# A decoder layer on eight cores: the ScalarE half of layer-norm jobs moved behind the next unit's PSUM copies, down partials added straight from PSUM, wide loads, and an fp16 copy of x1

## Chip, cores, metric

One Trainium2 chip, one program on all 8 cores, in two dies (cores 0 to 3 and 4 to 7). The metric is the device time of one execution in microseconds (us), on the slowest of the cores. Executions fall into two states: in the slow one a die has a visibly lower granted TensorE clock and the time is some per cent longer.

In the text, TensorE is the matmul engine (PE in the profile), VectorE is DVE, ScalarE is ACT, GpSimd is POOL. PSUM is the memory that the matmuls write, divided into banks; SBUF is the other memory on the chip, from which the engines work. In the profile lines `sp` is a PSUM bank and `arena` is SBUF. A line "PE sp L1295 <- ACT arena L1423" means that TensorE, at line 1295 of the kernel, waited for what ScalarE does at line 1423.

## The reference, cut to what matters

```python
def layer_norm(x, g, b):
    xf = x.astype(jnp.float32)
    mu = xf.mean(-1, keepdims=True)
    var = jnp.square(xf - mu).mean(-1, keepdims=True)
    return ((xf - mu) * lax.rsqrt(var + LN_EPS) * g + b).astype(x.dtype)

def swiglu(x, w_up, w_down):
    gate, up = jnp.split(jnp.einsum('bsd,df->bsf', x, w_up), 2, axis=-1)
    return jnp.einsum('bsf,fd->bsd', jax.nn.silu(gate) * up, w_down)

# reference(), one layer; SEQ = 16384, D_MODEL = 2048, D_FF = 5632
mix = token_mixer(x, ...)                         # attention, w_out
x = layer_norm(ALPHA * x + mix, ln1_g, ln1_b)     # "x1"
x = layer_norm(ALPHA * x + swiglu(x, w_up, w_down), ln2_g, ln2_b)
```

The change lies in what follows `token_mixer`: the two layer norms and the feed-forward product.

## The kernel before

A core has 2048 tokens and does the feed-forward part for two halves of 1024 (`st`), and in each half for two halves of the hidden width (`g`). One `(st, g)` has 22 **units**, each giving two 128x512 tiles of the hidden layer h, and then a **down stage** of eight **steps**, each giving 2 x 2 tiles of the output. So there are four down stages, in order: stage 1 (`st`=0, `g`=0) adds x1 to its products and stores the partial as `z2s`; stage 2 (0, 1) reads that partial back and finishes it; stages 3 and 4 do the same for the second half.

Products are done in half-size blocks, seven instead of eight, of sums of weights and of activations that VectorE makes: a unit is 7 x 8 = 56 matmuls into four PSUM banks, a step 7 x 11 = 77.

Between the units **jobs** are run, two in a unit: in `st` = 0 the last layer-norm operations of x1 for the second half, in `st` = 1 those of the output of the first half. There are 32 jobs in each half, so 16 units carry them. A job is two VectorE operations (subtract the mean, multiply by the inverse deviation) and one ScalarE operation (scale and bias), then a store:

```python
def ln1_tile(ss, st, n, hh, z, bz):
    ...
    S_.dve(lambda: nc.vector.tensor_tensor(out=z, in0=z, in1=mu, op=ALU.subtract), [bz, bmu], [bz])
    S_.dve(lambda: nc.vector.tensor_tensor(out=z, in0=z, in1=rs, op=ALU.mult), [bz, brs], [bz])
    ...
    S_.act(lambda: nc.scalar.activation(out=z, in_=z, **args), [bz, k.bsmall], [bz])
    S_.dma("act", k.x1s_d[n, :, c0:c0 + 512], z, [bz], [b], "x1s")
```

`S_.dve`, `S_.act` and `S_.dma` append to an engine's program; the lists are the buffers read and written, from which the waits follow. Each engine works through its program in order. A unit (cut):

```python
if fl == 0 and g == 0:
    ...                      # first unit of a half: 64 plain matmuls, then sums of x1 on VectorE
    run_jobs(2)
    continue
...
P("4", s, True, True)                                   # P: 8 matmuls into a bank
S_.act(lambda ...: nc.scalar.activation(out=v4, in_=pa, func=AF.Copy), [ba_], [b4])   # first copy
P("5", s + 1, True, True)
S_.act(lambda ...: nc.scalar.activation(out=v5, in_=pb, func=AF.Copy), [bb_], [b5])   # second copy
P("1", s + 2, True, True)
tt(v5, b5, pd, bd_, v5, b5, ALU.subtract)
P("2", s + 3, True, True)
tt(v4, b4, pc, bc_, v4, b4, ALU.add)
...                                                     # weight sums P, Q of the next unit
P("3", s + 1, False, True)     # adds to the bank of the second copy: must wait for it
...
if kh:
    ...                        # every second unit: four more sums, over h
...                            # weight sum R of the next unit
run_jobs(2)
```

A down step and the reload of x1 for the second half (cut):

```python
P("4", s, True, True, cs)
acc_x(*q21, pa, ba_)                       # q..: the loaded partial tiles, in SBUF
P("5", s + 1, True, True, cs)
S_.act(lambda pb=pb: nc.scalar.activation(out=t5, in_=pb, func=AF.Copy), [bb_], [bt5])
P("1", s + 2, True, True, cs)
tt(t5, bt5, pd, bd_, t5, bt5, ALU.subtract)
P("2", s + 3, True, True, cs)
tt(q21[0], q21[1], pc, bc_, q21[0], q21[1], ALU.add)
...
P("3", s + 1, False, True)
acc_x(*q12, pb, bb_)
P("7", s, False, True)
tt(t11, bt11, pa, ba_, t5, bt5, ALU.add)
acc_x(*q11, t11, bt11)                     # SBUF + SBUF
P("6", s + 3, False, True)
tt(t5, bt5, t5, bt5, pc, bc_, ALU.subtract)
tt(t5, bt5, pb, bb_, t5, bt5, ALU.add)
acc_x(*q22, t5, bt5)                       # SBUF + SBUF

def load_x1(st, b):                        # fp32 in DRAM, cast to fp16 by the transfer
    S_.dma("pool", xall[:, b, :, :], k.x1s_d[8 * kh:8 * kh + 8, :, c0:c0 + 512].rearrange("n p t -> p n t"), ...)
```

The softmax here doesn't subtract the row's maximum and nothing guards it: scores larger than these inputs give would overflow.

Of the kernel before, what the change touches and what calls it, by code (L numbers as in the profile page):

```python
# [8 lines left out]
F32 = mybir.dt.float32  # L9
# [3 lines left out]
ALU = mybir.AluOpType  # L13
# [202 lines left out]
def build(debug=False):  # L216
# [34 lines left out]
    k.x1s_d = dt("x1s", [KC, 128, TOK], F32, kind="Internal").ap()  # L251
    k.z2s_d = dt("z2s", [KC, 128, TOK], F32, kind="Internal").ap()
# [868 lines left out]
def phase3(k):  # L1121
# [73 lines left out]
    bx1s = {}  # L1195

    def ln1_tile(ss, st, n, hh, z, bz):
        (mu, bmu), (rs, brs) = ss["stat"][hh]
        S_.dve(lambda: nc.vector.tensor_tensor(out=z, in0=z, in1=mu, op=ALU.subtract), [bz, bmu], [bz])
        S_.dve(lambda: nc.vector.tensor_tensor(out=z, in0=z, in1=rs, op=ALU.mult), [bz, brs], [bz])  # L1200
        args = dict(func=AF.Identity, bias=k.lnp[:, 1, n:n + 1], scale=k.lnp[:, 0, n:n + 1])
        if st == 0:
            key = (RAW[n // 8, hh], n % 8)
            S_.act(lambda: nc.scalar.activation(out=xb[key], in_=z, **args), [bz, k.bsmall], [bxb[key]])
        S_.act(lambda: nc.scalar.activation(out=z, in_=z, **args), [bz, k.bsmall], [bz])
        b = Buf("x1s%d_%d_%d" % (st, n, hh))
        c0 = st * TS + hh * 512
        S_.dma("act", k.x1s_d[n, :, c0:c0 + 512], z, [bz], [b], "x1s")
        bx1s[(st, n, hh)] = b

    def load_x1(st, b):
        (kh, hh), = [e for e in RAW if RAW[e] == b]
        c0 = st * TS + hh * 512
        S_.dma("pool", xall[:, b, :, :], k.x1s_d[8 * kh:8 * kh + 8, :, c0:c0 + 512].rearrange("n p t -> p n t"),
               [bx1s[(st, n, hh)] for n in range(8 * kh, 8 * kh + 8)], [bxb[b, c] for c in range(8)], "x1l")

    fins = []
    jobs = []

    def run_jobs(n):  # L1220
        for _ in range(min(n, len(jobs))):
            jobs.pop(0)()

    for st in range(2):
# [19 lines left out]
        for si, (n, hh) in enumerate(steps):  # L1244
# [15 lines left out]
            if st == 1:  # L1260
                run_jobs(3 if si < 2 else 2 if si % 2 else 1)
                if not jobs:
                    wgate(k, 0, 0)
# [69 lines left out]
    for st in range(2):  # L1333
        for g in range(2):
# [7 lines left out]
                     [xslot(10), xslot(11), xslot(5), WB + 11264] + [WB + i * 2048 for i in range(4)]  # L1342
            zr = {}

            def load_xq(p):
                q = []
                for i in range(4):
                    n, hh = 2 * p + i // 2, i % 2
                    c0 = st * TS + hh * 512
                    o = zslots[4 * p + i] if last else wslot(6 - 4 * (p % 2) + i)  # L1350
                    v, b = slot("xq%d%d_%d_%d" % (st, g, n, hh), o)
                    if g == 0:
                        S_.dma("sp", v, k.x1s_d[n, :, c0:c0 + 512], [bx1s[(st, n, hh)]], [b], "xq")
                    else:
                        S_.dma("sp", v, k.z2s_d[n, :, c0:c0 + 512], [bz2s[(st, n, hh)]], [b], "xq")
                    q.append((v, b))
                    zr[n, hh] = (v, b)
                return q

            for fl in range(FG):  # L1360
# [4 lines left out]
                if fl == FG - 1:  # L1365
                    xq = load_xq(0)
# [15 lines left out]
                if fl == 0 and g == 0:  # L1382
# [19 lines left out]
                    run_jobs(2)  # L1402
                    continue
# [9 lines left out]
                S_.act(lambda v5=v5, pb=pb: nc.scalar.activation(out=v5, in_=pb, func=AF.Copy), [bb_], [b5])  # L1413
                P("1", s + 2, True, True)
# [29 lines left out]
                run_jobs(2)  # L1444
            assert not jobs

            t5, bt5 = slot("y5%d%d" % (st, g), wslot(0))
            t11, bt11 = slot("y11%d%d" % (st, g), wslot(1))
# [3 lines left out]
            def acc_x(v, b, o, bo):  # L1452
                if g == 0:
                    S_.dve(lambda: nc.vector.scalar_tensor_tensor(out=v, in0=v, scalar=ALPHA, in1=o, op0=ALU.mult, op1=ALU.add), [b, bo], [b])
                else:
                    S_.dve(lambda: nc.vector.tensor_tensor(out=v, in0=o, in1=v, op=ALU.add), [b, bo], [b])

            for p in range(KC // 2):
# [4 lines left out]
                (pa, ba_), (pb, bb_), (pd, bd_), (pc, bc_) = [(bank(k, s + i), k.bBK[s + i]) for i in range(4)]  # L1463
# [8 lines left out]
                if p == 0:  # L1472
                    for i, bk in (("4", s), ("5", s + 1), ("1", s + 2), ("2", s + 3)):
                        P(i, bk, True, False, range(NJ - 1))
                cs = [NJ - 1] if p == 0 else None
                P("4", s, True, True, cs)
                acc_x(*q21, pa, ba_)
                P("5", s + 1, True, True, cs)
                S_.act(lambda pb=pb: nc.scalar.activation(out=t5, in_=pb, func=AF.Copy), [bb_], [bt5])
                P("1", s + 2, True, True, cs)  # L1480
                tt(t5, bt5, pd, bd_, t5, bt5, ALU.subtract)
                P("2", s + 3, True, True, cs)
                tt(q21[0], q21[1], pc, bc_, q21[0], q21[1], ALU.add)
# [5 lines left out]
                P("3", s + 1, False, True)  # L1489
                wdone(k, key)  # L1490
                acc_x(*q12, pb, bb_)
                P("7", s, False, True)
                tt(t11, bt11, pa, ba_, t5, bt5, ALU.add)
                acc_x(*q11, t11, bt11)
                P("6", s + 3, False, True)
                if p == 7 and g == 0:
                    u_sums(st, FG, "Q")
                tt(t5, bt5, t5, bt5, pc, bc_, ALU.subtract)
                tt(t5, bt5, pb, bb_, t5, bt5, ALU.add)
                acc_x(*q22, t5, bt5)  # L1500
# [4 lines left out]
                for i, (v, b) in ((2, q21), (1, q12), (0, q11), (3, q22)):  # L1505
                    n, hh = 2 * p + i // 2, i % 2
                    c0 = st * TS + hh * 512
                    if g == 1:
                        stats(ss, hh, v, b)
                    if not last:  # L1510
                        bz2s[(st, n, hh)] = Buf("z2s")
                        S_.dma("sp", k.z2s_d[n, :, c0:c0 + 512], v, [b], [bz2s[(st, n, hh)]], "z2o")
                if st == 0 and g == 1:
                    if p == 0:
                        open_x(1)
                    if 1 <= p <= 4:
                        load_x1(1, (B11, B22, B12, B21)[p - 1])
                xq = nxq
            if g == 1:
                so = [xslot(6 + i) if last else wslot(6 + i) for i in range(4)]  # L1520
                ss.update(stat=[[slot("mu%dl" % hh, so[hh]), slot("rs%dl" % hh, so[2 + hh])] for hh in range(2)], tt=[slot("ttl", wslot(1))])
# [6 lines left out]
                def ln2_tile(ss, zr, st, n, hh, idx):  # L1528
# [5 lines left out]
                    else:  # L1534
# [3 lines left out]
                    S_.act(lambda: nc.scalar.activation(out=z, in_=z, func=AF.Identity, bias=k.lnp[:, 3, n:n + 1], scale=k.lnp[:, 2, n:n + 1]),  # L1538
                           [bz, k.bsmall], [bz])
                    b = Buf("out%d_%d_%d" % (st, n, hh))  # L1540
                    final.append(S_.dma("act", k.outT_d[n, :, c0:c0 + 512], z, [bz], [b], "of%d" % (idx % 6)))
# [4 lines left out]
    while jobs:  # L1546
        jobs.pop(0)()
# [132 lines left out]
```

## Time and profile before

| | before |
|---|---|
| median of 3 runs | 3262.33 us (3262.0 to 3478.6) |
| spans of the cores, profiled run | 3228.3 to 3258.8 us, slowest core 2 |
| mean granted clock, by core | 0.946 to 0.951 |
| start of the feed-forward part, core 2 | 1347.9 us |
| units 3 to 17 of a half (with jobs), mean of cores | 262.5 and 260.8 us, 17.5 and 17.4 each |
| second unit of a half (with jobs) | 24.0 and 24.1 us |
| units without jobs | 12.1 us each |
| down stages 1 to 4, mean of cores | 143.5, 167.6, 140.6, 133.4 us |
| stage 2 by core, 0 to 7 | 163, 159, 178, 164, 159, 178, 163, 177 us |

The rows from the third on come from the trace: the 7408 matmuls of the feed-forward line, in order of their start, cut into pieces of 64 (the first unit of a half), 56 (units) and 77 (steps), each lasting from the start of its first matmul to the start of the next piece's first. The jobs stand at the end of units 1 to 16 and their ScalarE work delays the unit behind, so units 2 to 17 are slow. The fifteen units from the third to the seventeenth are the "fifteen job units" of the prediction; the second unit is listed by itself because it is much longer. The profile lines of before stand in the prediction.

### The profile page before, as it was taken

The numbers are of one execution on the slowest core, as the hardware profiler recorded it, in microseconds if no ns is written. First come the engines' busy times: TensorE is split into PE (matmuls) and PEld (weight loads), VectorE is DVE, ScalarE is ACT, GpSimd is POOL, SyncE is SP. The second block draws the span as 40 slices with busy tenths as digits, with TensorE's granted clock in tenths as the row PEclk, the third lists the DMA queues.
The fourth block names the chain that finished last, engine by engine and source line by source line (L and its number), as shares of the span: only waits on it lengthen the run. The fifth ranks groups of instructions, "written<-read, shape, count | busy, mean of one in ns | idle before, by whom it ended". The sixth has DMA issues, their size and how long they took to land.

```text
span 3258.8 us, 41848 instructions; the slowest of 8 cores (3228.3 to 3258.8 us)
## 1 busy us (share of the span) xinstructions
PE 2847.1 (87%) x14965; PEld 1341.8 (41%) x15077; DVE 2036.6 (62%) x2688; ACT 735.8 (23%) x1059; POOL 660.8 (20%) x604
## 2 busy tenths in 40 slices
PE   5999996998885888787799999986877899999993
PEld 2445553445554333333344444432333344444441
DVE  0556544886775748466666567664666666576687
ACT  0000001664553126222220012211222210112114
POOL 2000000452333576500000000044200000000173
PEclk8999998999997999988999999998989899999997
DMA  9951114155447479644457844589456568655653
GB/s 169 161 123 61 59 43 99 40 121 120 109 104 182 97 142 191 125 91 93 91 107 183 178 83 86 100 171 185 111 124 120 118 115 192 148 91 91 133 126 103
DMA packets 209229, 390.13 MB, mean 120 GB/s; under 512 B 88448, under 2 KB 110336, under 8 KB 192128
## 3 DMA queue, kind: packets, MB, share of 16 engines
q0 software_dynamic: 35984, 194.82, 35.6%
q1 hardware_dynamic: 154608, 159.06, 17.7%
q10 hardware_dynamic: 18432, 33.56, 2.9%
q8 instruction: 123, 2.02, 0.3%
q14 instruction: 82, 0.67, 0.1%
HBM read 496.67 MB, written 85.52 MB: 179 GB/s over the span
## 4 chain that ended last, share of the span: by engine, by line
PE 60%; DVE 14%; DMA 14%; issue 6%; ACT 3%; SPq 1%; POOL 1%; ACTq 0%; DVEq 0%; another core or an unknown queue 0%; POOLq 0%
PE sp L1282 37%; PE sp L482 7%; PE sp L469 6%; DMA z2s<-arena 4%; DMA arena<-xres 4%; PE sp L703 4%; DVE arena L1379 2%; PE sp L1115 2%; DVE arena L851 1%; DMA arena<-x1s 1%; DMA arena<-z2s 1%; DVE arena L1536 1%; DMA arena<-wv 1%; DVE arena L1303 1%; DVE arena L1537 1%
## 5 line engine op out<-in xcount | busy, mean ns | idle before, releaser
L1282 PE MATMUL sp<-arena 128*128 128x512 f16 x7408 | 1672.0, 390 | 173.4 <-ACT arena L1413 123.0
L1282 PEld LDWEIGHTS sp<-arena 128*128 128x128 f16 x7408 | 737.6, 100 | 1108.0 <-issue 283.2
L1379 DVE TENSOR_TENSOR arena<-sp,arena 128x512 f32<-128x512 f32 (+1 forms) x476 | 324.5, 690 | 406.2 <-PE sp L1282 301.8
L139 POOL DMA_DIRECT2D arena<-wup x88 | 46.7, 531 | 1177.7 <-PE sp L1282 601.1
L1115 PE MATMUL sp<-arena 128*128 128x512 bf16 x1002 | 234.2, 393 | 40.8 <-DVE arena L1266 31.9
L703 PE MATMUL sp<-arena 128*128 128x512 bf16 x976 | 229.1, 385 | 26.4 <-DMA arena<-wq 11.6
L469 PE MATMUL sp<-arena 128*128 128x384 bf16 (+1 forms) x1161 | 212.5, 344 | 10.4 <-DMA arena<-xT 9.8
L482 PE MATMUL sp<-arena 128*128 128x512 bf16 x1001 | 220.1, 379 | 1.2
L1158 POOL TENSOR_TENSOR arena<-arena 128x512 f32<-128x512 f32 x120 | 186.3, 1553 | 114.9 <-DVE arena L1379 48.5
L1115 PEld LDWEIGHTS sp<-arena 128*128 128x128 bf16 x1024 | 102.1, 101 | 173.1 <-issue 63.3
L451 DVE TENSOR_TENSOR arena<-sp,arena 128x384 bf16<-128x384 f32 (+1 forms) x81 | 47.8, 605 | 200.5 <-PE sp L469 105.1
L1159 POOL TENSOR_TENSOR arena<-arena 128x512 f32<-128x512 f32 x120 | 169.8, 1415 | 6.7 <-ACT arena L1157 6.7
L1303 DVE TENSOR_TENSOR arena<-arena 128x2048 f16<-128x2048 f16 (+1 forms) x118 | 163.0, 1381 | 0.0
L1157 ACT ACTIVATE arena<-arena 128x512 f32<-128x512 f32 x120 | 75.6, 630 | 375.1 <-DVE arena L1379 108.1
L469 PEld LDWEIGHTS sp<-arena 128*128 128x128 bf16 x1168 | 114.7, 98 | 106.6 <-issue 13.6
L1295 DVE TENSOR_TENSOR arena<-arena 128x2048 f16<-128x2048 f16 (+1 forms) x118 | 157.0, 1331 | 2.0 <-DMA arena<-wdn 2.0
L357 ACT ACTIVATE arena<-sp,arena 128x512 bf16<-128x512 f32 (+1 forms) x37 | 25.1, 679 | 587.1 <-PE sp L502 443.6
L703 PEld LDWEIGHTS sp<-arena 128*128 128x128 bf16 x1024 | 98.7, 99 | 142.5 <-issue 33.4
L1379 DVE TENSOR_TENSOR arena<-arena 128x512 f16<-128x512 f32 (+1 forms) x304 | 154.7, 569 | 0.0
L482 PEld LDWEIGHTS sp<-arena 128*128 128x128 bf16 x1024 | 100.3, 98 | 120.2
L1379 DVE TENSOR_TENSOR arena<-arena,sp 128x512 f32<-128x512 f32 x118 | 81.0, 687 | 101.0 <-PE sp L1282 100.8
L1376 ACT ACTIVATE arena<-sp 128x512 f32<-128x512 f32 x90 | 53.5, 597 | 355.1 <-PE sp L1282 355.1
(123 smaller groups left out, 2619.3 us busy)
## 6 DMA issues: line engine op xcount, KB each, us to landing
arena<-wup POOLq DMA_DIRECT2D x88, 1024.0 KB, 8.9
arena<-wdn POOLq DMA_DIRECT2D x32, 1408.0 KB, 14.2
z2s<-arena SPq DMA_DIRECT2D x96, 256.0 KB, 10.6
arena<-z2s SPq DMA_DIRECT2D x96, 256.0 KB, 6.3
arena<-wout POOLq DMA_DIRECT2D x32, 512.0 KB, 8.3
arena<-xres SPq DMA_DIRECT2D x64, 256.0 KB, 5.8
x1s<-arena ACTq DMA_DIRECT2D x64, 256.0 KB, 3.3
arena<-x1s SPq DMA_DIRECT2D x64, 256.0 KB, 6.7
```

Source lines behind the costliest of these rows:

```text
L469: ins = nc.tensor.matmul(bank(k, bk)[:, 0:c1 - c0], x[:, kc, blk * 128:blk * 128 + 128], wv[:, kc, c0:c1], start=(kc == 0), stop=(kc == KC ...
L482: ins = nc.tensor.matmul(bank(k, bk), wk[h][:, kc, :], x[:, kc, :], start=(kc == 0), stop=(kc == KC - 1))
L703: ins = nc.tensor.matmul(bank(k, bk), w[:, kc, :], x[:, kc, :], start=(kc == 0), stop=(kc == KC - 1))
L1115: ins = nc.tensor.matmul(bank(k, bk), w[:, kc, :], y[:, kc, hh * 512:(hh + 1) * 512], start=(first and i == 0), stop=(last and i == len(kc ...
L1157: S_.act(lambda: nc.scalar.activation(out=sq, in_=z, func=AF.Square), [bz], [bsq])
L1158: S_.pool(lambda: nc.gpsimd.tensor_tensor(out=za, in0=za, in1=z, op=ALU.add), [bz, bza], [bza])
L1159: S_.pool(lambda: nc.gpsimd.tensor_tensor(out=qa, in0=qa, in1=sq, op=ALU.add), [bsq, bqa], [bqa])
L1282: ins = nc.tensor.matmul(bank(k, bk), w, x, start=(first and i == 0), stop=(last and i == len(ws) - 1), skip_group_check=True)
L1295: S_.dve(lambda: nc.vector.tensor_tensor(out=v, in0=w[:, 0:n, :], in1=w[:, n:2 * n, :], op=ALU.add), [bw], [b])
L1303: S_.dve(lambda: nc.vector.tensor_tensor(out=v, in0=w[:, :, 0:128], in1=w[:, :, 128:256], op=ALU.subtract), [bw], [b])
L1376: S_.act(lambda: nc.scalar.activation(out=o, in_=i, func=AF.Silu), [bi], [bo])
L1379: S_.dve(lambda: nc.vector.tensor_tensor(out=o, in0=a, in1=b, op=op), [ba, bb], [bo])
```

## The change

Its intent: take ScalarE's share of the jobs out of the ring TensorE, VectorE, ScalarE, TensorE in each unit; shorten the down step's work on VectorE and ScalarE; halve the number of transfers; and give stage 2 less to load. Cut to its core:

```diff
 def ln1_tile(ss, st, n, hh, z, bz):          # ln2_tile likewise
     S_.dve(... subtract ...)
     S_.dve(... mult ...)
-    S_.act(lambda: nc.scalar.activation(out=z, in_=z, **args), [bz, k.bsmall], [bz])
-    S_.dma("act", k.x1s_d[n, :, c0:c0 + 512], z, [bz], [b], "x1s")
+    def rest():
+        S_.act(lambda: nc.scalar.activation(out=z, in_=z, **args), [bz, k.bsmall], [bz])
+        S_.dma("act", k.x1s_d[n, :, c0:c0 + 512], z, [bz], [b], "x1s")
+        if st == 1:
+            S_.dma("pool", k.x1h_d[RAW[n // 8, hh], :, n % 8, :], z, [bz], [b], "x1h")   # fp16 copy
+    acts.append(rest)

-def load_x1(st, b):
-    S_.dma("pool", xall[:, b, :, :], k.x1s_d[8 * kh:8 * kh + 8, :, c0:c0 + 512].rearrange(...), ...)
+def load_x1(b):
+    S_.dma("sp", xall[:, b, :, :], k.x1h_d[b], ...)

 # first unit of a half
     run_jobs(2)
+    run_acts()
     continue
 # other units
     S_.act(... copy v5 ...)
+    run_acts()
     P("1", s + 2, True, True)
     ...
     run_jobs(2)
+    if fl == 17:
+        xq = load_xq(0)                      # was at fl == 21

 # load_xq and the z2s stores: one transfer of 1024 columns (512 KB) in place of two of 512 (256 KB)
-    S_.dma("sp", v, k.z2s_d[n, :, c0:c0 + 512], [bz2s[(st, n, hh)]], [b], "xq")
+    if hh:
+        S_.dma("sp", v, src[n, :, st * TS:(st + 1) * TS], [bs[(st, n, e)] for e in range(2)], ..., "xq")

 # down step
-    P("4"); acc_x(q21, pa); P("5"); ACT copy to t5; P("1"); t5 = pd - t5; P("2"); q21 += pc
+    P("5"); P("1"); P("4")
+    q11 -= BB; q22 -= BB; q11 += BD; q22 += BD; q21 += BA      # each from its PSUM bank
+    P("2"); q21 += BC
     P("3")
-    acc_x(q12, pb); P("7"); t11 = pa + t5; q11 += t11; P("6"); t5 -= pc; t5 += pb; q22 += t5
+    q12 += BB; q22 += BB; P("7"); q11 += BA; P("6"); q22 -= BC
```

The last lines are shorthand for the calls.

## The prediction

> **What bounds the kernel now.** I read the page first: the span is 3258.8 us on the slowest core, TensorE is busy for 87% of it, and in the chain that ended last the matmul line L1282 (all products of the feed-forward part) carries 37%. So a gain must come from TensorE waiting less in that part. Next I read who waited for whom on TensorE from 1300 us to the end, then the busy times of each engine stage by stage, and last the timeline of one slow unit.
>
> Waits of TensorE (us in all, times, longest):
>
> ```profile
> PE sp L1282 <- ACT arena L1413: 123.0, 32, 7.4
> PE sp L1282 <- DVE arena L1456: 35.6, 3, 22.4
> PE sp L1282 <- DVE arena L1454: 10.6, 6, 3.8
> ```
>
> The first wait comes 32 times. 32 is also the number of feed-forward units that carry layer-norm jobs: 16 in the first token half (stores of x1 for the second half), 16 in the second (output of the first half). Nothing else is of that size.
>
> Busy time by stretch (us; PE, PEld, DVE, ACT, POOL; then clock, DMA share, GB/s). In order: fifteen job units, down products 1, twenty-two units without jobs, down products 2, fifteen job units, down products 3, the last down products:
>
> ```profile
> 1380.00:1645.00 265.00, 208.12 (x840) 87.23 (x840) 164.47 (x243) 61.09 (x94) 7.94 (x15) 0.89 0.43 93
> ...
> 1713.00:1857.00 144.00, 136.37 (x618) 60.65 (x616) 79.59 (x100) 5.34 (x9) 4.22 (x8) 0.98 0.84 187
> 1857.00:2123.00 266.00, 266.00 (x1235) 120.54 (x1233) 182.30 (x260) 52.70 (x88) 11.62 (x22) 1.00 0.51 94
> 2123.00:2301.00 178.00, 141.91 (x618) 61.99 (x617) 99.23 (x99) 23.88 (x40) 93.83 (x71) 0.88 0.87 174
> ...
> 2335.00:2597.00 262.00, 207.65 (x840) 87.06 (x840) 163.76 (x242) 59.08 (x90) 7.93 (x15) 0.89 0.55 118
> ...
> 2664.00:2803.00 139.00, 134.94 (x616) 60.28 (x615) 79.78 (x100) 4.81 (x9) 4.22 (x8) 0.99 0.86 193
> ...
> 3069.00:3205.00 136.00, 134.52 (x620) 60.50 (x618) 101.65 (x102) 24.21 (x40) 93.16 (x65) 1.00 0.51 116
> ```
>
> A unit is 56 matmuls. With jobs it takes 265/15 = 17.7 us (later 262/15 = 17.5); without, 266/22 = 12.1. A down step is 77 matmuls, 16.6 us at full rate, so eight take 133. The four down stages take 144, 178, 139 and 136.
>
> One job unit in the timeline (start, us, engine):
>
> ```profile
> 1415.14 0.69 DVE L1200 TENSOR_TENSOR arena<-arena 128x512 f32<-128x512 f32 x1
> 1415.42 0.33 ACTq L139 DMA_DIRECT2D x1s<-arena  x1
> 1415.93 0.81 ACT L1205 ACTIVATE arena<-arena 128x512 f32<-128x512 f32 x1 [0.58 <-DVE arena L1200]
> 1416.82 0.33 ACTq L139 DMA_DIRECT2D x1s<-arena  x1
> 1417.24 0.60 ACT L1411 ACTIVATE arena<-sp 128x512 f32<-128x512 f32 x1 [0.50 <-ACT arena L1205]
> 1417.74 0.59 ACT L1413 ACTIVATE arena<-sp 128x512 f32<-128x512 f32 x1
> 1418.43 1.29 DVE L1379 TENSOR_TENSOR arena<-sp,arena 128x512 f32<-128x512 f32 x2 [2.60 <-ACT arena L1413]
> 1418.44 0.34 PEld L1282 LDWEIGHTS sp<-arena 128*128 128x128 f16 x3 [3.06 <-issue]
> 1418.47 13.93 PE L1282 MATMUL sp<-arena 128*128 128x512 f16 x56 [2.60 <-ACT arena L1413]
> ```
>
> VectorE ends the previous unit's jobs, ScalarE then does their second half (L1205), only then the two PSUM copies of this unit (L1411, L1413), and the matmul that reuses the bank of the second copy starts last. So each unit is a closed ring of TensorE, VectorE and ScalarE.
>
> **What the Trainium skill says.** "TensorE: Matmul & The Clock Gate", Part 1: The HAM clock gate, has TensorE fall to half rate after an idle window of about 3.4 us and recover after a busy one. The trace agrees: on all cores the granted clock is only 0.5 or 1.0, in pieces of whole multiples of 3.413 us, and the stretch with jobs has mean 0.89, the one without 1.00. A wait therefore costs more than its own length. "VectorE: DVE Perf Modes", Why PSUM operands drop a tier, puts fp32 with a PSUM operand at the plain rate. In this trace it costs nothing extra: the fp32 subtraction with PSUM takes 690 ns, the same size within SBUF 692 (L1537). "SBUF — State Buffer", SBUF: two separate sides, says a VectorE operation with two SBUF inputs and a GpSimd operation can lock each other out. It fits: the accumulation L1456 takes 1615 ns from SBUF, 683 from PSUM, while GpSimd sums statistics. "DMA: Bandwidth & Descriptors", Issuing engines are not separate DMA queues: all queues share the same 16 engines, so moving the x1 reload to another queue gains only by what it no longer moves.
>
> **The change part by part.**
>
> Deferred ScalarE half. No work is removed: two operations of 0.81 us per job unit now stand behind both copies. The third-bank matmul then needs only its copy, 0.60 us after the product, with two products (3.4 us) in between, as in units without jobs. VectorE work stays: 164.5/15 = 10.96 us per unit, against 8.29 without jobs, in a unit of 12.1. It is 91% full. I checked the tightest wait in the program order: the sixth product's bank must have been read by VectorE, which comes behind the old jobs. In the slower kind of unit (with the sums over h) VectorE goes on 8.6 us after the last product (1425.7 to 1434.2 in the timeline), plus two PSUM additions of 0.69 makes 9.9; the matmul is due 6 x 1.72 = 10.3 us after. It fits by some 0.3 us. I allow 0.2 us a unit for slips, so 12.3. Gain: 15 x (17.67 - 12.3) + 15 x (17.47 - 12.3) = 81 + 78 = 159 us. The first full unit of each half (22.4 and 24.3 us) loses its wait of up to 7.4 us but then waits some 2.7 us for VectorE, which still has fresh sums to make: I take 5 each, 10 together. Sum 169, a little above the 123 us of wait because the half-rate stretches go too.
>
> Down partials from PSUM. Per step nine VectorE additions and a ScalarE copy become ten additions at 0.69 us; with 4.5 us of weight sums that is 11.4 of 16.6 us. VectorE is not the end here, so the count gives nothing by itself. In stages 2 and 4 two SBUF accumulations per step go, which spares VectorE 2 x 0.93 us, off the path. The last result is ready some 2 us earlier (one operation after the last product instead of three), but the old partial must now be there earlier: its bank is wanted at the fifth product (9.4 us less two additions, 8.0) instead of the sixth (about 11.1). These nearly cancel: 0.
>
> Wide transfers. Same bytes, half as many. In the packet records a 2 KB packet takes 84 ns in the median, a 4 KB one 159: 5% less per byte. The first loads, three units earlier, were in time already (17.3 us first steps everywhere). Stages 1 and 3 lose 11 and 6 us over 133 now; I give 2 us each, 4 together.
>
> The fp16 copy. It bears on stage 2 alone, where the x1 reload (4 x 1024 KB, cast on the way, 18.9 us each) comes on top: 178 us against 133, and two waits of VectorE for z2s there, 27 us the longest. The cast packets are 4096 of 1 KB at a mean 120 ns, 31 us of all 16 engines. As 512 packets of 8 KB without a cast I estimate 11 to 15 us, from the 84 to 121 ns of a 2 KB packet. So 15 to 20 us of a DMA load at 0.87 of 178 = 155 us go, and it then looks like stage 1 with 12 us more: I keep 17 us of the 44, a gain of 27 on this core. Cores whose stage 2 is now 158 to 164 us gain about 12, but start from spans of 3228 to 3245, so all cores end near each other. The copy's 32 writes lie in job units; with them DMA is busy an estimated 9 of 12.3 us there.
>
> Sum: 169 + 0 + 4 + 27 = 200. The timed median is 3262.3, so about 3063 us.
>
> **Rivals.** (a) VectorE becomes the bound of the job units. For: 91% full, a margin of 0.3 us, descriptors for the x1 copy made on GpSimd beside it. If each unit slips 1.2 us, 30 us return: 3093. Against: its backlog is under a unit and drains at 1.1 us a unit. (b) The DMA stays the bound of the down stages, or grows worse because writes wait for both halves and the reload shares their queue. For: DMA share 0.84 to 0.87 there with rates of 174 to 193 GB/s. Stage 2 then stays at 178: 3090. If everything is hidden instead, all three stages run at 133 and the time falls to some 3035. (c) The clock: longer dense stretches might bring on a lower granted clock. For: one of the three timed runs was 3478.6 us. Against: 266 us of unbroken matmuls run at 1.00 here. Were such a state usual now, the gain would be lost; I give it 2%.
>
> **Range and chances.** Both large terms can miss by 30 us, mostly towards longer: 3035 to 3100. Even (a) and (b) together (3120) stay over 4% faster. Faster 0.96, within 2% 0.03, slower 0.01.
>
> **What would show it.** Right: the wait of TensorE for the copy L1413 falls from 123 us to under 5, job units last 12.1 to 12.5, the clock there is near 1.00, stage 2 near 150 us, stages 1 and 3 hardly change, the tail after the last product stays about 54 us. Wrong: TensorE waits for VectorE additions in job units, stage 2 stays over 165, or a granted clock between 0.5 and 1.0.

## More of the kernel before

The weights of the steps go in turn into three places of a ring; the last two steps use them in the order 1, 0:

```python
U_OFF = [WB, WB + 8192, WB + 16384]
D_OFF = [WB + (24576, 13312, 0)[i] for i in (0, 1, 2, 0, 1, 2, 1, 0)]
```

## The result, and the profile after

| | before | after |
|---|---|---|
| median (4 runs each) | 3262.16 us (3254.98 to 3478.6) | 3071.34 us (3063.74 to 3075.66) |
| ratio | | 0.942 (95%: 0.939 to 0.945) |
| spans of the cores | 3228.3 to 3258.8 | 3056.4 to 3074.3, slowest core 0 |
| granted clock, by core | 0.946 to 0.951 | 0.964 to 0.967 |

A ratio is the mean time of one kernel's fast runs over that of the other's fast runs of the same rounds, so it is not quite the ratio of the medians. The result was correct, and so was that of every run below.

First the waits of TensorE in the kernel after, from 1300 us to the end on its slowest core (us in all, times, longest):

```profile
PE sp L1295 <- ACT arena L1423: 14.9, 2, 7.4
PE sp L1295 <- DVE arena L1470: 13.2, 4, 5.8
PE sp L1295 <- DVE arena L1468: 13.1, 5, 5.0
...
PE sp L1295 <- DVE arena L1308: 3.6, 2, 1.9
```

The matmul line is now L1295, the second copy L1423, the additions of the down steps L1468 and L1470. The wait for the second copy came 32 times and took 123 us; it now comes twice, and each time it has its old length, 7.4 us. So it was taken away in thirty units and not touched in two. In the kernel before, on core 2, these thirty waits make 108 us. Units 3 to 17 got shorter by 160 us together; the other 52 us go with the half clock, which that core had for 113 us of these units.

The busy times by stretch on core 0 (columns as in the prediction), in order: fifteen job units, down stage 1, twenty-two units without jobs, down stage 2, fifteen job units, down stage 3, down stage 4:

```profile
1387.00:1568.00 181.00, 181.00 (x832) 81.45 (x831) 157.47 (x236) 59.10 (x88) 22.87 (x43) 0.99 0.81 148
1635.00:1777.00 142.00, 134.85 (x617) 60.40 (x615) 85.12 (x110) 0.10 (x1) 4.22 (x8) 0.99 0.79 187
1777.00:2043.00 266.00, 266.00 (x1234) 120.54 (x1232) 180.81 (x258) 53.05 (x88) 11.61 (x22) 1.00 0.50 94
2043.00:2193.00 150.00, 137.67 (x616) 60.80 (x615) 105.97 (x109) 19.78 (x32) 82.13 (x66) 0.95 0.87 205
...
2235.00:2417.00 182.00, 182.00 (x845) 82.34 (x843) 161.46 (x242) 60.42 (x90) 7.91 (x15) 1.00 0.81 164
2477.00:2619.00 142.00, 136.04 (x617) 60.76 (x616) 85.29 (x110) 0.20 (x1) 4.21 (x8) 0.98 0.79 187
2885.00:3019.00 134.00, 132.97 (x616) 60.00 (x615) 102.98 (x109) 19.48 (x32) 86.59 (x64) 1.00 0.53 119
```

Fifteen job units take 181 us instead of 265 and 262. TensorE is busy in all of it, at clock 0.99 and 1.00 instead of 0.89: a job unit is now as fast as one without jobs. VectorE has the same work in it (157 us against 164), but in a shorter time. Down stage 2 is 150 us, with DMA still busy 87% of it; stages 1, 3 and 4 are as they were.

Inside one job unit of core 0 (start, us, engine) the new order can be read:

```profile
1503.95 0.60 ACT L1421 ACTIVATE arena<-sp 128x512 f32<-128x512 f32 x1 [0.80 <-PE sp L1295]
...
1505.68 0.60 ACT L1423 ACTIVATE arena<-sp 128x512 f32<-128x512 f32 x1 [1.13 <-PE sp L1295]
...
1507.91 0.81 ACT L1208 ACTIVATE arena<-arena 128x512 f32<-128x512 f32 x1 [1.64 <-DVE arena L1201]
...
1509.31 0.82 ACT L1208 ACTIVATE arena<-arena 128x512 f32<-128x512 f32 x1 [0.58 <-DVE arena L1201]
```

Both copies (L1421, L1423) wait for nothing but the matmuls that fill their banks. The jobs' ScalarE operations (L1208) come after them and wait for VectorE, and none of TensorE's waits after 1300 us is put down to them.

The whole of the gain can be laid out on the slowest cores, core 2 before and core 0 after, from the same cutting of the trace (us):

| | before, core 2 | after, core 0 | difference |
|---|---|---|---|
| to the start of the feed-forward part | 1347.9 | 1350.1 | +2.2 |
| first units | 37.6 | 36.3 | -1.3 |
| second units | 46.7 | 48.4 | +1.7 |
| units 3 to 17, both halves | 523.1 | 363.1 | -160.0 |
| other units (no jobs) | 652.6 | 652.6 | 0 |
| down stages 1 and 3 | 283.3 | 284.2 | +0.9 |
| down stage 2 | 177.8 | 150.3 | -27.5 |
| down stage 4 | 133.4 | 134.1 | +0.7 |
| after the last product | 56.1 | 55.1 | -1.0 |
| span | 3258.8 | 3074.3 | -184.5 |

(Sums may be off by 0.3 from rounding.) Two rows make the result. The row of stage 2 compares two different cores: core 2 by itself went from 178 to 144 us, and the mean of the cores from 167.6 to 147.4.

### The profile page after: what moved, and what is told of

Same layout as the page of the kernel before. It is cut to its first block, busy times and chain, and to the rows that moved or that the text cites. A ratio compares the mean times of both kernels' runs of the same rounds, so it can differ in the third digit from the quotient of the medians.

```text
span 3074.3 us, 41686 instructions; the slowest of 8 cores (3056.4 to 3074.3 us)
## 1 busy us (share of the span) xinstructions
PE 2795.6 (91%) x15077; PEld 1329.0 (43%) x15077; DVE 2048.3 (67%) x2720; ACT 721.1 (23%) x1027; POOL 661.7 (22%) x632
## 4 chain that ended last, share of the span: by engine, by line
PE 69%; DMA 13%; DVE 11%; issue 3%; ACT 2%; POOL 1%; SPq 1%; another core or an unknown queue 0%; DVEq 0%; ACTq 0%; POOLq 0%
PE sp L1295 47%; PE sp L483 7%; PE sp L470 7%; DMA arena<-xres 5%; PE sp L704 4%; DMA z2s<-arena 3%; DVE arena L852 2%; DVE arena L1105 1%; DMA arena<-wv 1%; PE sp L1116 1%; DMA arena<-ys 1%; DMA arena<-z2s 1%; DMA arena<-x1s 1%; DVE arena L346 1%; ACT arena L843 1%
## 5 line engine op out<-in xcount | busy, mean ns | idle before, releaser
L1295 PE MATMUL sp<-arena 128*128 128x512 f16 x7408 | 1616.2, 381 | 45.0 <-ACT arena L1423 14.9
L1295 PEld LDWEIGHTS sp<-arena 128*128 128x128 f16 x7408 | 726.8, 98 | 934.5 <-issue 73.2
L1388 DVE TENSOR_TENSOR arena<-sp,arena 128x512 f32<-128x512 f32 (+1 forms) x348 | 236.7, 688 | 176.9 <-PE sp L1295 156.8
L1116 PE MATMUL sp<-arena 128*128 128x512 bf16 x1024 | 238.9, 397 | 37.9 <-DVE arena L1279 30.6
L1470 DVE TENSOR_TENSOR arena<-arena,sp 128x512 f32<-128x512 f32 x256 | 166.7, 681 | 135.0 <-PE sp L1295 112.9
L704 PE MATMUL sp<-arena 128*128 128x512 bf16 x1024 | 236.5, 385 | 20.8 <-DMA arena<-wq 11.1
L483 PE MATMUL sp<-arena 128*128 128x512 bf16 x1024 | 222.2, 379 | 0.0
L1316 DVE TENSOR_TENSOR arena<-arena 128x2048 f16<-128x2048 f16 (+1 forms) x118 | 189.0, 1602 | 0.0
L1159 POOL TENSOR_TENSOR arena<-arena 128x512 f32<-128x512 f32 x120 | 170.0, 1416 | 74.1 <-DVE arena L1279 43.2
L1160 POOL TENSOR_TENSOR arena<-arena 128x512 f32<-128x512 f32 x120 | 173.5, 1446 | 6.2 <-ACT arena L1158 6.0
L1308 DVE TENSOR_TENSOR arena<-arena 128x2048 f16<-128x2048 f16 (+1 forms) x118 | 156.2, 1324 | 1.3 <-DMA arena<-wdn 1.3
L1421 ACT ACTIVATE arena<-sp 128x512 f32<-128x512 f32 x86 | 51.4, 598 | 433.8 <-PE sp L1295 432.8
## 6 DMA issues: line engine op xcount, KB each, us to landing
arena<-wdn POOLq DMA_DIRECT2D x32, 1408.0 KB, 14.1
z2s<-arena SPq DMA_DIRECT2D x48, 512.0 KB, 10.4
```

The source lines that it names most:

```text
L483: ins = nc.tensor.matmul(bank(k, bk), wk[h][:, kc, :], x[:, kc, :], start=(kc == 0), stop=(kc == KC - 1))
L704: ins = nc.tensor.matmul(bank(k, bk), w[:, kc, :], x[:, kc, :], start=(kc == 0), stop=(kc == KC - 1))
L1116: ins = nc.tensor.matmul(bank(k, bk), w[:, kc, :], y[:, kc, hh * 512:(hh + 1) * 512], start=(first and i == 0), stop=(last and i == len(kc ...
L1159: S_.pool(lambda: nc.gpsimd.tensor_tensor(out=za, in0=za, in1=z, op=ALU.add), [bz, bza], [bza])
L1160: S_.pool(lambda: nc.gpsimd.tensor_tensor(out=qa, in0=qa, in1=sq, op=ALU.add), [bsq, bqa], [bqa])
L1295: ins = nc.tensor.matmul(bank(k, bk), w, x, start=(first and i == 0), stop=(last and i == len(ws) - 1), skip_group_check=True)
```

## The experiments

Three sets were run, each on one chip with its own runs of the kernel before; the record calls it chip 1 for the first and third set and chip 2 for the second. The fast runs of the first and third set are like those above. Chip 2 granted a lower clock in parts of all four runs that were profiled there. The second and third set have the changed kernel as control. The first set (defer_only, no_defer, cast_reload, narrow) has none; there the comparison is with the change's profile and runs above, so small differences in the timed value should not be read from it. The medians are of all runs of a kernel, slow ones included; where two kernels are compared in us, the mean of the fast runs is given. "Stages" are means over the 8 cores of one profiled run.

### defer_only: the deferral alone, on the kernel before

```diff
-    S_.act(...); S_.dma("act", ...)
+    def rest():
+        S_.act(...); S_.dma("act", ...)
+    acts.append(rest)
     ...
+    run_acts()        # at the same places as in the change
```

> The kernel before with the deferral of the ScalarE half alone. Theory (the deferral and the end of the half-rate clock after it make most of the gain): the fifteen job units of each half last 12.1 us instead of 17.6, the unit just after the first stays at 22 to 25 us, the four down stages stay as before (144, 158 to 178, 139, 133). Time 3262 less 160: about 3100 us. Rival (the shorter units push the weight transfers together, and only the other parts made room for them): job units over 12.5 us, time over 3125.

Measured: ratio 0.947 (0.943 to 0.951), median 3092.09 us; three of its five runs were at 3078 to 3092, two slow. Units 3 to 17 take 181.3 and 181.5 us, the same as with the whole change. Stages: 139.6, 162.8 (157.0 to 173.0), 140.9, 133.4 us. So the deferral alone gives the whole gain of the job units, 160 us. The stages differ from those before by no more than the spread between cores (stage 1 before: 139.7 to 148.2). What it lacks is stage 2. The wait left there on its slowest core, core 4, is this one (waits of TensorE from 1300 us; L1291 is the matmul, L1468 the addition of a partial loaded from DRAM):

```profile
PE sp L1291 <- DVE arena L1468: 29.8, 2, 24.6
```

### no_defer: all the rest of the change, without the deferral

```diff
-    acts.append(rest)
+    rest()
```

> The changed kernel with the ScalarE half back at the end of its job. Theory: job units last 17.6 us again, TensorE waits some 120 us for the second PSUM copy, the down stages stay as in the changed kernel (about 141, 147, 141, 134): 3071 plus 160 to 165, about 3233 us. Rival (the parts overlap in what they gain): under 3215 or over 3250.

Measured: ratio 0.990 (0.986 to 0.994), median 3223.12 us. Units 3 to 17: 259.7 and 261.1 us, as before the change; stages 139.3, 147.1, 139.0, 134.1, as after it. Its wait for the second copy, read as above, has come back whole:

```profile
PE sp L1295 <- ACT arena L1423: 123.1, 32, 7.4
```

So the two halves of the change act in different stretches of the kernel. By the ratios, 5.3% for the deferral and 1.0% for the rest make 6.3%, against 5.8% together; with intervals of 0.3 to 0.4 to either side that is not clearly different.

### cast_reload: the change without the fp16 copy

```diff
-            if st == 1: S_.dma("pool", k.x1h_d[...], z, ...)          # no fp16 copy is written
-        S_.dma("sp", xall[:, b, :, :], k.x1h_d[b], ...)
+        S_.dma("pool", xall[:, b, :, :], k.x1s_d[8 * kh:8 * kh + 8, :, c0:c0 + 512].rearrange("n p t -> p n t"), ...)
```

> The changed kernel with x1 of the second half reloaded from its fp32 copy, cast on the way, by the GpSimd queue; no fp16 copy. Theory (the fp16 copy relieves the second down stage of DMA time): that stage goes from 144 to 151 us back to 158 to 178, the others do not move: 3085 to 3100 us. Rival (stage 2 fell because of the PSUM additions and the wide transfers): within 5 us of 3071.

Measured: ratio 0.947 (0.943 to 0.952), median 3092.05 us. Stages: 140.3, 159.3 (152.4 to 163.8), 139.9, 134.1. Stage 2 is 12 us longer than with the copy, and the rest is unchanged, so the fp16 copy is worth 12 us in the mean of the cores. The other two parts, in this kernel and not in defer_only, took stage 2 from 162.8 to 159.3, within the spread between cores. The 12 us are read from the trace, where the two kernels' cores do not overlap (144.2 to 151.2 with the copy); in the timed value the intervals of this run and of the change (0.939 to 0.945) overlap.

What the copy changes can be seen in the DMA view of stage 2 (output name <- input, queue, KB each, median us from issue to landing; first line: packets, MB and share of the 16 engines). Before, core 2:

```profile
q0 software_dynamic: 5448, 15.90, 55.4%
...
arena<-x1s POOLq DMA_DIRECT2D x4, 1024.0 KB, 18.9
```

After, core 0:

```profile
q0 software_dynamic: 1296, 11.80, 45.6%
...
arena<-x1h SPq DMA_DIRECT2D x4, 1024.0 KB, 15.6
```

The reload keeps its four transfers, but the queue that also brings the weights loses some 4150 packets. The reload itself is quicker by only 3 us each. VectorE's waits for the partials show where the gain lies: in stage 2, in the mean of the cores, they are 44.1 us before, 27.3 in cast_reload and 18.1 with the copy, and TensorE's waits are 27.3, 19.8 and 10.4. The run puts back three things at once, the cast with its small packets, the fp32 source and the queue of the weights. Which of them costs the 12 us was not tested.

### narrow: the change with transfers of 512 columns

```diff
-    if hh: S_.dma("sp", v, src[n, :, st * TS:(st + 1) * TS], ...)      # and the same for the stores
+    S_.dma("sp", q[-1][0], src[n, :, c0:c0 + 512], ...)
```

> The changed kernel with 256 KB loads and stores of the partial sums instead of 512 KB, at the same places in the program. Theory (same bytes at nearly the same rate, DMA bound by bytes): within 6 us of 3071, down stages within 3 us each. Rival (half as many transfers, or the later store of the first half of each pair, decides when the next partial can be loaded): stages 1 to 3 move by over 5 us each, so 3085 or more, or 3057 or less if the early small stores were the better ones.

Measured: ratio 0.948 (0.943 to 0.953), median 3084.57 us. Stages 144.2, 152.0, 142.5, 134.1: some 3.5, 4.6 and 0.9 us longer than in the change. That is more than the theory allowed and less than the rival asked for; the fast runs' mean is 3087 against 3071. Against the kernel before, wide transfers won nothing clear in stages 1 and 3 (143.5 and 140.6 there). A reading that fits, but is not shown: the new order of additions wants all of the old partial early and without wide transfers pays for this. The old order with narrow transfers was run only together with other differences (before, defer_only: 139.6 in stage 1).

### after_again: the changed kernel, on the second chip

The kernel is the changed one, unaltered.

> The changed kernel once more, as the control of this set: 3064 to 3076 us, stages as in its first profile (about 141, 147, 141, 134 us).

Measured: ratio 0.956 (0.953 to 0.959), median 3201.84 us against 3355.29. Both kernels are slower on this chip, the changed one by 130 us and the one before by 93. The clock view, which is for the whole run:

```profile
core 2: 3209.3 us, clock 0.917
...
core 4: 3156.6 us, clock 0.930
```

So 3064 to 3076 us was missed. The record of core 2 has a granted clock of 0.8125 for 922 us, cores 0, 4 and 6 for 741, 718 and 659 us. It comes in pieces, on core 0 of 15 us with some 10 us at 1.0 between them. Two neighbouring cores (0 and 1, 2 and 3, 4 and 5, 6 and 7) have the same pieces at the same times after their start; other pairs, on the same die too, have different ones. In the first profile of the changed kernel no core has that value, only 1.0 and 0.5. Job units take 13.4 us here, and units without jobs 12.8 and 13.0. So on this chip a lower clock takes back a part of the gain. A tighter kernel spends more of its time at TensorE's rate and would pay more for a slower one; that is a reading, as the kernel before was not profiled on this chip. The relative comparison of the next three runs holds against this control.

### old_acc: the change with the old order of products and additions in the down steps

```diff
-    P("5"); P("1"); P("4"); q11 -= BB; q22 -= BB; ...
+    P("4"); acc_x(q21, pa); P("5"); S_.act(... copy to t5 ...); P("1"); t5 = pd - t5; ...
```

> The changed kernel with the down partials combined as before (ScalarE copy, two temporaries, the old order of the four first products); all else stays. Theory (VectorE is not the end in the down stages, what the earlier last result gains the earlier need of the old partial takes away): within 6 us of the control; first steps 17.3 instead of 17.7 us. Rival A (adding straight from PSUM frees VectorE in stages 2 and 4 and that counts): 8 us or more slower, in stage 2. Rival B (the earlier need of the old partial causes the wait of the seventh step): 8 us or more faster, the seventh steps under 20 us.

Measured: ratio 0.9562 (0.9535 to 0.9588), the control 0.9561. Stages 144.7, 154.1, 148.7, 144.4 against 146.7, 155.1, 146.7, 144.6 in the control: nothing either way. Here adding from PSUM is worth nothing in time. At the full clock of chip 1 it was not tried by itself; a slower TensorE leaves VectorE and the loads more time, so the 0 is shown for chip 2 only. (In this run the last stage also has the old places of its buffers, and two of its loads are narrow.) Rival B came half true: the seventh steps fall below 20 us (18.5, 19.9 and 18.0 against 19.9, 23.5 and 19.8), but the eighth ones rise (18.8, 21.0 and 22.0 against 18.4, 18.7 and 18.4). The kernel before, with the same order, has its long steps there too (20.1 and 22.8 us for the seventh and eighth step of stage 1). So the order moves the wait for the old partial by one step.

It does move something, though. In the groups of instructions of stage 2 (busy us, mean ns of one | idle before), first old_acc on core 3:

```profile
L1473 DVE TENSOR_TENSOR arena<-arena 128x512 f32<-128x512 f32 x16 | 29.9, 1869 | 1.7 
L1316 DVE TENSOR_TENSOR arena<-arena 128x2816 f16<-128x2816 f16 x7 | 12.4, 1767 | 0.0
```

and the changed kernel on core 0:

```profile
L1470 DVE TENSOR_TENSOR arena<-arena,sp 128x512 f32<-128x512 f32 x79 | 50.7, 680 | 42.3 <-PE sp L1295 21.1 <-DMA arena<-z2s 20.4
...
L1316 DVE TENSOR_TENSOR arena<-arena 128x2816 f16<-128x2816 f16 x8 | 31.3, 3907 | 0.0
```

With the old order the additions within SBUF (L1473) take 1869 ns while GpSimd makes its sums of statistics. With the new order no addition is slow (680 ns each, from PSUM), but the weight sum L1316, which has both inputs in SBUF, takes 3907 ns instead of 1767 (on chip 2, in after_again, 4750 to 4900 on cores 0, 2 and 3). In stage 1, where GpSimd has no such sums, the same L1316 takes 1618 ns. The delay was not removed but handed on to the next operation of that kind.

### swap: the seventh step's weights in the place that is free first

In the changed kernel the seventh step of stages 1 to 3 takes 22.8, 25.5 and 23.6 us, where a step at full rate takes 16.6. The timeline of stage 1 on core 2 shows why (start, us, engine):

```profile
1706.09 1.05 POOL L139 DMA_DIRECT2D arena<-wdn  x2 [32.71 <-PE sp L1295]
...
1722.83 9.01 SPq L139 DMA_DIRECT2D arena<-x1s  x2
...
1738.41 0.69 DVE L1468 SCALAR_TENSOR_TENSOR arena<-arena,sp 128x512 f32<-128x512 f32 x1 [9.10 <-DMA arena<-x1s]
```

Two weight loads of 1408 KB are issued back to back, because the one in front (seventh step) waits for the place of the fifth, and the eighth's, behind it in the same queue, goes at once. The load of the partial (x1s) comes behind both and is late for the addition.

```diff
-D_OFF = [WB + (24576, 13312, 0)[i] for i in (0, 1, 2, 0, 1, 2, 1, 0)]
+D_OFF = [WB + (24576, 13312, 0)[i] for i in (0, 1, 2, 0, 1, 2, 0, 1)]
```

> The changed kernel with the weight places of the seventh and eighth down step exchanged, so that the seventh's load can start one step earlier and not together with the eighth's. Theory (the 6 to 8 us wait in the seventh step of stages 1 to 3 is the old partial waiting behind two weight loads issued back to back): seventh steps fall to 17 to 19 us, 12 to 20 us off the time: about 3055 us. Rival (the DMA engines are full over the whole stage): the wait moves to another step or to the first units of the next stage, under 5 us off.

Measured: ratio 0.9607 (0.957 to 0.964) against 0.9561 for the control, and a mean of the fast runs of 3218 against 3203 us: the gain that was expected did not come. The seventh steps fall to 17.5, 18.7 and 17.8 us (control 19.9, 23.5, 19.8), but the first unit after stages 1 and 3 rises to 18.1 and 17.7 us (12.7 and 12.8): its weights now have to wait for the last step's place. VectorE's waits for partials in stages 1 to 3 go from 8.9, 5.7 and 7.7 us to 0, 0.9 and 0. So the cause of the long seventh step was right, but the wait only moved, as the rival said. Why the timed runs are even slower is not shown: the profiled run is the fastest of them and not slower than the control's.

### shift: no jobs in the first unit of a half

```diff
                     run_jobs(2)          # removed, in the first unit only
                     run_acts()           # removed
```

> The changed kernel without layer-norm jobs in the first unit of each half; the sixteen pairs of jobs start one unit later. Theory (the second unit of each half lasts 23 to 24 us because the first unit's jobs still run their ScalarE half before its PSUM copies, and then VectorE is behind): second units 13 to 16 us, 16 to 20 us off the time: about 3053 us. Rival (the fresh sums on VectorE alone hold the second unit): it stays over 19 us, under 10 us off.

The second unit of each half is where the wait of 7.4 us stayed. In the timeline of the changed kernel on core 0, second half (ScalarE and TensorE only):

```profile
2223.20 0.81 ACT L1556 ACTIVATE arena<-arena 128x512 f32<-128x512 f32 x1 [12.81 <-DVE arena L1553]
2224.60 0.81 ACT L1556 ACTIVATE arena<-arena 128x512 f32<-128x512 f32 x1 [0.58 <-DVE arena L1553]
2225.94 0.60 ACT L1421 ACTIVATE arena<-sp 128x512 f32<-128x512 f32 x1 [0.52 <-ACT arena L1556]
2226.43 0.59 ACT L1423 ACTIVATE arena<-sp 128x512 f32<-128x512 f32 x1
2227.17 9.15 PE L1295 MATMUL sp<-arena 128*128 128x512 f16 x28 [7.45 <-ACT arena L1423]
```

Here the jobs' ScalarE operations (L1556) still stand ahead of the copies: the first unit calls `run_acts()` right after its own `run_jobs(2)`, and VectorE comes to those jobs only after all the fresh sums. Without jobs in the first unit there is nothing to wait for; the sixteen pairs then end one unit later.

Measured: ratio 0.9518 (0.9495 to 0.9541), mean of the fast runs 3189 against 3203 us for the control: 13 us, a little less than the 16 to 20 expected. The second unit takes 14.5 and 14.1 us instead of 23.8 and 23.5. (The profile of this run fell into the slow state; the second units are so much shorter that this does not matter, and its other stretches are not used.)

### after_third: the changed kernel, on the chip of the third set

The kernel is the changed one, unaltered.

> The changed kernel as the control of this set. If this chip grants TensorE the full clock in dense stretches, 3064 to 3076 us with dense units of 12.1 us; if it grants 13/16 in parts of them as in the set before, about 3200 us with dense units near 13 us.

Measured: ratio 0.945 (0.940 to 0.950), median 3065.13 us; second units 23.9 and 23.6, stages 140.0, 146.8, 139.7, 134.1. The kernel before was often slow in this set (median 3371.53 of 11 runs, the fastest 3238.76), so its ratios are wide; the kernels of this set are better compared with one another.

### shift_swap2: both cures, with the units' weight places moved to fit

```diff
-U_OFF = [WB, WB + 8192, WB + 16384]
-D_OFF = [WB + (24576, 13312, 0)[i] for i in (0, 1, 2, 0, 1, 2, 1, 0)]
+U_OFF = [WB, WB + 24576, WB + 13312]
+D_OFF = [WB + (24576, 13312, 0)[i] for i in (0, 1, 2, 0, 1, 2, 0, 1)]
                     run_jobs(2)          # removed, in the first unit only
                     run_acts()           # removed
```

> The candidate for a better version: no jobs in the first unit of each half, the seventh and eighth down weights exchanged, and the three places of the up weights moved so that the first two of the next stage no longer lie under the eighth down weights. Theory: second units 14 to 15 us (24 in the control), seventh steps 17 to 19 us, first units of the next stage 12 to 13 us and not 18 as with the exchange alone: 25 to 35 us under the control. Rival (the DMA work of a down stage cannot be fitted in at all, so a wait only moves): second units fall, but the down stages and the units after them together gain under 5 us: 15 to 20 us under the control.

Measured: ratio 0.934 (0.931 to 0.937), median 3034.69 us; the mean of the fast runs is 3033 against 3069 for after_third on the same chip, 36 us less. The second units take 14.1 and 14.0 us, stages 1 to 4 134.2, 144.2, 134.9 and 133.9, the seventh steps 16.6, 17.2 and 16.6; the first units after stages 1 and 3 are 13.7 and 14.4 instead of 12.1. In the profiles the first and second units thus give 21 us, stages 1 to 3 give 13, and the units behind them take back 4. The wait for L1423 is gone from its list, with 4.7 us (two waits) for the first copy, L1421, in its place. This version beats both kernels.

### vec1 and vec2: more VectorE work in the job units

One (vec1) or two (vec2) multiplications of 128 x 448 fp32 into scratch, after the first job's own, in every unit with jobs but the first; they take 618 to 622 ns each in the trace.

```diff
     S_.dve(... mult ...)                 # of the first job
+    for _ in range(1):                   # vec2: range(2)
+        S_.dve(lambda: nc.vector.tensor_tensor(out=pad_o, in0=mu[:, 0:448], in1=mu[:, 0:448], op=ALU.mult), [bmu], [bpad])
```

> The changed kernel with one more VectorE operation (448 columns, near 0.6 us) in fifteen of the job units of each half. Theory (VectorE has 1.1 us of room per unit on average and 0.2 to 0.4 us at the tightest wait): units of the slower kind lose 0.2 to 0.5 us, 3 to 8 us in all. Rival (there is more room than I worked out): no unit moves.

> The same with two more VectorE operations a unit, near 1.2 us. Theory: VectorE has 10.96 plus 1.2 = 12.2 us of work in a unit of 12.1 and becomes the bound: units of 12.4 to 13 us, 10 to 25 us in all. Rival: no unit moves, under 3 us in all.

Measured: vec1 ratio 0.945 (0.941 to 0.949), median 3070.27 us; its job units take 184.0 and 184.4 us for fifteen, 12.3 each (12.1 in the control). vec2 ratio 0.951 (0.943 to 0.959), its fast runs between 3076 and 3111 us; job units 189.9 us in the second half, 12.7 each. (In its first half two cores ran at a lower clock, 211.5 us; the other six took 190.2.) Now TensorE does wait for VectorE in the job units; the waits list has a new line that comes 16 times, in eight of the fifteen units of each half. On core 0, first vec1, then vec2:

```profile
PE sp L1302 <- DVE arena L1395: 3.3, 16, 0.5
...
PE sp L1302 <- DVE arena L1395: 15.0, 16, 1.3
```

The single units show the rest. Every second unit (the one behind a unit with the sums over h) goes from 12.09 to mostly 12.43 us with one extra operation and mostly 13.16 with two; those between stay at 12.09. So the first extra 0.62 us costs 0.34 us in such a unit, a margin of 0.62 - 0.34 = 0.3 us, and the second costs 0.73.

## Why the prediction was right, and where it was not

**The deferral, units 3 to 17: right.** It predicted 12.3 us a unit and 159 us in all; it is 12.1 and 160.0, and defer_only and no_defer show that the deferral alone does it. The allowance of 0.2 us for slips was not needed. The clock went with it, from 0.89 to 0.99 and 1.00 in those stretches, as the step said.

**The first full unit of each half: this step failed.** The prediction put it so: it "loses its wait of up to 7.4 us but then waits some 2.7 us for VectorE [...]: I take 5 each, 10 together". It lost nothing: 46.7 us for both before, 48.4 after. The reason was to be read in the diff: `run_acts()` stands directly behind `run_jobs(2)` in the unit before it, so that there nothing is deferred. The wait list (twice 7.4 us), the timeline and the run shift show it. Together they gained nothing of the 10 us; in the table above, where 200 us were predicted and 184.5 came, that is 11.7 of the missing 15.5. Stages 1 and 3, 4.9 us short, are the other part. The timed median, 3071 against 3063, is closer than that. Without jobs in the first unit the second one is shorter by 9.7 us a half (shift_swap2), twice what was predicted; but that also takes those jobs' VectorE work out of the first unit, so it is not the same step.

**The wait "under 5 us"** is by the same reason 14.9.

**Down partials from PSUM: right at 0, as far as tried** (old_acc 0.9562, control 0.9561, at the lower clock of chip 2). But the sub-step that two SBUF accumulations a step "go, which spares VectorE 2 x 0.93 us" was wrong: VectorE is busy 106.0 us in stage 2 of core 0, against 99.2 before on core 2, since the weight sum took over the delay. It lay off the path, as was said, so it cost nothing.

**Wide transfers and early loads, 4 us: a little too much.** Stages 1 and 3 went from 143.5 and 140.6 to 140.7 and 141.6 in the mean, 2 us together, and defer_only has 139.6 and 140.9 without any wide transfer. What narrow loses (9 us over the three stages) is no gain over before. The excess of stages 1 and 3 over 133 lay elsewhere: in the old partial that comes late behind the weight loads of the last two steps, which the prediction did not look into. With those places changed (shift_swap2) the stages take 134.2 and 134.9 us.

**The fp16 copy: right on the slowest core, with parts mixed.** Stage 2 was to fall from 178 to 150; it is 150.3 on the slowest core after, 147.4 in the mean. On the other cores about 12 us were expected; 163, 159, 164, 159 and 163 (cores 0, 1, 3, 4 and 6) became 150, 145, 150, 145 and 150, 14 us. The 27 us are in part luck, as they compare core 2 before with core 0 after; the cores that took 178, 178 and 177 us (2, 5 and 7) came to 144, 151 and 144. Of the mean fall of 20 us the copy by itself makes 12 (cast_reload); 5 lie between the kernel before and defer_only, and 3.5 are the other parts, these two within the spread between cores. The reasoning by the packets was sound in direction: DMA is busy for 0.87 of the stage before and after, and the stage got shorter.

**The rivals.** (a) VectorE as the bound did not come; vec1 and vec2 find the margin of some 0.3 us that was worked out, in every second unit. (b) The DMA as bound of stage 2 holds in part: 147 us against 133 is left. (c) The lower clock came as the usual state on chip 2 only, where the saving was 4.4% instead of 5.8%, not nil. The changed kernel was not slow more often: none of its 16 timed runs was slow, against 16 of 37 of the kernel before and 15 of 54 of the variants.

**Open.** Why chip 2 granted 0.8125 in every profiled run was not found; the kernel is the same. On chip 1 that value stands in one profile only, vec2, on cores 6 and 7 for 158 us; no slow run of chip 1 is among the kept profiles. Why stage 2 keeps 10 us over stages 1 and 3 even in shift_swap2 (144.2 against 134.2 and 134.9) was not taken apart. Nor was the seventh step of stage 2 tried by itself without the reload of x1.

## What to carry to other kernels

In a ring of engines it matters more what stands ahead of an operation in its engine's own program than how long that operation is: two operations of 0.81 us in front of a copy, which themselves wait for VectorE, cost 5 us a unit, and behind it nothing. When such a reordering is checked, read it at the edges too, in the first turn of the loop, where the deferred list may be run at once. And a wait list with counts (32 times, then 2 times) tells both that it worked and where it did not.

## What the Trainium skill lacked or had wrong

- "TensorE: Matmul & The Clock Gate", Part 1: The HAM clock gate, states a limiter that takes a whole die to 13/16 of the clock once three of its cores run dense matmuls. With eight cores in 266 us of unbroken matmuls the profiles before and after show 1.00 (stretch 1777 to 2043 of core 0 after) and no 0.8125 on any core. On chip 2 exactly this value stands for 659 to 952 us of a run, by pairs of cores and not by the whole die, in pieces (median of a core 6 to 15 us) with the full clock between them. The page gives it for the default power profile; which one these chips had is not recorded.
- "SBUF — State Buffer", SBUF: two separate sides, describes the port that VectorE (two SBUF inputs) and GpSimd share, and the runs agree: 680 ns from PSUM, 1869 ns from SBUF, for the same addition. What it lacks is the consequence that taking one such operation out of the contention hands the delay to the next: the fp16 weight sum went from 1767 to 3907 ns, and VectorE's busy time in the stage did not fall.
- No page has the order within one in-order engine as a cost by itself: 1.6 us of ScalarE work ahead of a PSUM copy made a unit of 12.1 us take 17.4, three times its own length, because that work waits for VectorE in its turn and because of the half clock that followed TensorE's wait (108 us of wait and 52 us with the clock in thirty units).
